# Two layers of a hybrid encoder on one core: x laid out by halves, the vectors loaded later, the first norm's sums on TensorE, factors spread by transposes

## The chip, the core and the metric

The kernel runs on one core of a Trainium2 chip. A core has TensorE (PE in the profile; PEld is its loading of stationary operands), VectorE (DVE), ScalarE (ACT), GpSimd (POOL) and SyncE (SP, which here only issues transfers). They run side by side and wait for each other through semaphores; each takes its instructions in order. Matmul results land in PSUM, which has eight banks of 128 x 512 f32 numbers; everything else lives in SBUF, with 128 partitions.

The metric is the time of one execution on the device in microseconds (us). Before the change it is 1564.54 us, the median of 3 runs (1564.0 to 1566.41).

## What is computed

```python
for l in range(DEPTH):                       # 2 layers, x is 512 tokens x 1024
    h = rms_norm(x, g_pre_mix[l])
    proj = h @ w_in[l]                       # 1024 -> 5632
    q_a, k_a, v_a, q_b, k_b, v_b, q_m, gate_pre = jnp.split(proj, splits, axis=-1)
    o_a = neighborhood_attention(..., rpb_na[l])      # 6 heads on an 8 x 64 grid
    o_b = dilated_attention(...)                      # 6 heads, three dilations
    o_m = memory_attention(..., mem_n, w_mem_kv[l])   # 4 heads over 256 memory tokens
    gates = jax.nn.sigmoid(gate_pre.reshape(B, S, N_BRANCH, D) + b_gate[l])
    merged = (gates[:, :, 0] * (o_a @ w_br_a[l]) + gates[:, :, 1] * (o_b @ w_br_b[l])
              + gates[:, :, 2] * (o_m @ w_br_m[l]))
    x = x + rms_norm(merged @ w_out[l], g_post_mix[l])
    h = rms_norm(x, g_pre_ffn[l])
    u = depthwise_conv_centred(h @ w_up[l], conv_w[l], conv_b[l])   # 1024 -> 2 x 2816, width 3
    a, b = jnp.split(u, 2, axis=-1)
    x = x + rms_norm((jax.nn.gelu(a) * b) @ w_down[l], g_post_ffn[l])
```

`mem_n` is the memory after a norm of its own. All numbers are float32.

## The kernel before

**Layout.** Everything is held transposed: features on the 128 partitions, the 512 tokens along the row. x is eight blocks (k = 0 to 7) of 128 features, in two tiles of 128 x 4 x 512. The tokens fall into two halves of 256 (`HALVES`).

**Products.** Each f32 operand is split into a high part in the type fp32r and the remainder (lo). A product is then three matmuls that add into one bank: hi by hi, hi by lo, lo by hi (`mm3`). A weight tile of 128 x 1024 (512 KB) is fetched by SP into `wraw` (three buffers), ACT casts its high part (`whi`), and DVE, or POOL where the call says `G`, subtracts to get the remainder (`wlo`). Tiles kept for later lie in the pools `m`, `h` and `ka`.

**Order.** The program's order on PE is written by a planner (`Woven`): the main loop emits projections, and jobs written as generators (norms, attention heads, the ends of sublayers) are spawned with a delay and run their next step when the planner's clock, advanced by a cost per matmul, has passed their due time. An instruction of a job therefore stands between the matmuls of the main loop. The other engines take their instructions in the order in which this one program emits them.

**Norms.** Squares are made on ACT, summed over k on DVE, and the sum over partitions is a product with `mean`, a column of 1/1024, so that tokens come to lie on the partitions (`rstd_job`). ACT takes the root, DVE the reciprocal. To bring the factor back onto a row of tokens for all partitions, the column is repeated 128 times as a stationary operand and multiplied with the identity in f32, 128 tokens at a time (lines 334 to 337); the profile shows two records for each such product. 18 such jobs run. `normed` then scales x by the gain (a column of `vec`) and the factor, and splits it.

**The start.** SP fetches the first half of x in four transfers, two weight tiles, the second half of x, and more weights. POOL's queue fetches the identity (`ident`) and the table `vec` of all gains, biases and convolution weights (128 x 464, 237 KB). `first_squares` makes eight squares of a half and sums them on DVE in two chains, so that PE gets two mean products of 256 tokens.

**The first projections of each layer.** Six of them (`FIRST`) run half by half in pairs (`run_group`), because the second half's norm is not done yet. `group_banks` gives the banks: the first pair in mm banks, the second in s banks, the third in the banks o and pt.

**Between the layers.** While layer 0's down projection runs, `mem_norm_job` prepares the memory norm of layer 1: eight squares on ACT, summed on POOL. The keys and values of the memory and the first projections of layer 1 follow. `end_job` closes a sublayer: it scales the result, adds it to x, and squares and sums the new x for the next norm.

**Values of the first attention.** `a_v` copies a projection from PSUM into a rearranged tile: one copy on ACT and two small ones on DVE, ahead of four transposes on PE. It runs six times.

Of the kernel before, what the change touches and what calls it, by code (L numbers as in the profile page):

```python
# [7 lines left out]
F32 = mybir.dt.float32  # L8
# [111 lines left out]
def tile_hybrid_encoder(ctx, tc, xT, memT, memg, vecs, rpb, w_in, w_kv, w_bra, w_brb, w_brm,  # L120
# [65 lines left out]

    xs = [const.tile([128, 4, 512], F32, name=f"x{i}") for i in range(2)]
    x = [xs[k // 4][:, k % 4, :] for k in range(KD)]

    def load_x(half):  # L190
        for k in range(0, KD, 2):
            nc.sync.dma_start(out=xs[k // 4][:, k % 4:k % 4 + 2, half], in_=xT[:, k:k + 2, half])

    load_x(HALVES[0])
    eps = const.tile([128, 1], F32, name="eps")
# [8 lines left out]
    vec = const.tile([128, depth, V_N], F32, name="vec")  # L204
    nc.gpsimd.dma_start(out=vec, in_=vecs)
    mg = const.tile([128, KD], F32, name="mg")
# [152 lines left out]
    def pre_norm_job(l, goff, acc, hs, i):  # L359
        half, box = HALVES[i], []  # L360
        yield from rstd_job(acc if isinstance(acc, list) else [acc[:, half]], 256, box)
        for k in range(KD):
            normed(x[k][:, half], vec[:, l, goff + k:goff + k + 1], box[0], hs[k][0][:, half], hs[k][1][:, half],
                   G if k in LOG[l > 0 and goff == V_PRE] else V)
# [8 lines left out]
    def end_job(l, goff, og, acc, acc2, i, then, lat, more=()):  # L373
# [3 lines left out]
        for k in range(KD):  # L377
            V.tensor_mul(og[k][:, half], og[k][:, half], box[0])
            (G if then is None and i and k in TAILG else V).tensor_add(x[k][:, half], x[k][:, half], og[k][:, half])
            if acc2 is not None:  # L380
                sumsq_add(acc2[:, half], x[k][:, half], k == 0, None, G if k in SQG[goff == V_POSTF] else V)
            else:
                nc.sync.dma_start(out=out[:, k, half], in_=x[k][:, half])
        if then is not None:
# [3 lines left out]
    def factor_end_job(l, goff, og, acc, acc2, i, nxt):  # L388
# [5 lines left out]
        for k in range(KD):  # L394
            V.tensor_mul(og[k][:, half], og[k][:, half], box[0])
            V.tensor_add(x[k][:, half], x[k][:, half], og[k][:, half])
            raw_split(l, gnext, k, x[k][:, half], h[k][0][:, half], h[k][1][:, half])
            if k == 0:
                yield 0.6
            wv.give(f"h{l}.{gnext}.{i}.{k}")  # L400
            yield 1.05
        for k in range(KD):
            sumsq_add(acc2[:, half], x[k][:, half], k == 0)
        yield 3.5
# [58 lines left out]
    def group_banks():  # L463
        return [mmbank(), mmbank(), sbank(), sbank(), obank(128), tbank()]

# [76 lines left out]
    def a_v(ps, qkv, flag):  # L542
# [282 lines left out]
    def first_squares(half):  # L825
        sqs = [ytile((128, 256)) for _ in range(KD)]
        for k in range(KD):
            ACT.activation(sqs[k], x[k][:, half], AF.Square)
# [21 lines left out]
    for l in range(depth):  # L850
# [8 lines left out]
        for pr in range(3):  # L859
            for i, evac in enumerate((a_q, a_k, a_v)):  # L860
                ps = pss[3 * pr + i] if pr < 2 else proj(l, 3 * i + pr, hs, fence if i < 2 else None)
                evac(ps, qkva, *([f"va{l}.{pr}"] if i == 2 else []))
# [143 lines left out]
def _layout(inputs):  # L1006
# [12 lines left out]
    a = {}  # L1019
    a["xT"] = np.ascontiguousarray(g["x"][0].T.reshape(KD, 128, SEQ).transpose(1, 0, 2))  # L1020
    a["memT"] = np.ascontiguousarray(g["mem"][0].T.reshape(KD, 128, N_MEM).transpose(1, 0, 2))
# [45 lines left out]
```

## Time and profile before

| | |
|---|---|
| median of 3 runs | 1564.54 us (1564.0 to 1566.41) |
| the profiled execution | 1565.1 us |
| its span in the profile | 1563.3 us, so 1.8 lie around it |
| mean granted clock of PE | 0.994 |
| ACT, DVE, POOL busy | 47%, 60%, 10% |
| moved by DMA | 144.90 MB, mean 93 GB/s |

All views below are of this one execution. Times count from the start of the span. A row of a timeline gives start and length of a run of equal instructions, the engine, the line of the program (L114 is the helper through which ACT and DVE are called, L242 the one for matmuls), the operation, destination and sources by their names in the program, the size, and the count. In brackets stands how long the engine had been idle just before, and what ended that. The granted clock is PE's, as a share of full speed.

### The profile page before, as it was taken

The page shows a single profiled execution, that of the slowest core. Times are in us where ns is not written, and L with a number is a line of the kernel's source. Part 1 is how long each engine was busy: PE and PEld are TensorE (multiplying, and loading weights), DVE is VectorE, ACT ScalarE, POOL GpSimd, SP SyncE. Part 2 cuts the span into 40 slices and gives each one's busy share as a digit, 9 for nine tenths or more (in the row PEclk, how much of TensorE's full clock was granted, in tenths as well). Part 3 has the DMA queues.
Part 4 walks back from the last instruction along what each step waited for, and adds up shares of the span by engine and source line. Part 5 has one row for each costly group of instructions (what it writes and reads, how often), then busy time and mean ns, then how long its engine had stood idle before and what let it go on. Part 6 is the DMA issues. An engine that isn't in the chain of part 4 may idle for free.

```text
span 1563.3 us, 20698 instructions
## 1 busy us (share of the span) xinstructions
PE 1524.4 (98%) x7994; PEld 1303.7 (83%) x7994; DVE 945.2 (60%) x1682; ACT 735.1 (47%) x1267; POOL 155.2 (10%) x219
## 2 busy tenths in 40 slices
PE   6999999999999999999989999999999999999997
PEld 6888888888988888788889888888889888888887
DVE  6685566235777777742385856753456877775233
ACT  5564575236544444522344645743364544444231
POOL 4340000210000000100061400001100000000000
PEclk9999999999999999999989999999999999999999
DMA  7222113325113322333331221132250222333331
GB/s 244 88 79 72 61 57 96 93 95 163 54 56 101 100 94 95 104 98 101 115 115 44 80 69 63 56 108 81 95 189 15 81 95 95 94 100 96 98 103 63
DMA packets 46610, 144.90 MB, mean 93 GB/s; under 512 B 5232, under 2 KB 11376, under 8 KB 46512
## 3 DMA queue, kind: packets, MB, share of 16 engines
q1 hardware_dynamic: 44656, 139.61, 28.2%
q10 hardware_dynamic: 1152, 2.10, 0.5%
q0 software_dynamic: 704, 1.88, 0.4%
q8 instruction: 62, 1.02, 0.3%
q14 instruction: 36, 0.29, 0.1%
HBM read 141.47 MB, written 2.10 MB: 92 GB/s over the span
## 4 chain that ended last, share of the span: by engine, by line
PE 54%; DVE 3%; issue 0%; ACT 0%; ACTq 0%; DVEq 0%
PE mm L242 48%; PE s L242 3%; PE o L242 2%; PE pt L242 1%; PE pt L253 1%; DVE y L114 1%; DVE x L114 1%; DVE m L114 0%; DVE acc L114 0%; DVE wlo L114 0%; DVE ka L114 0%; DVE st L114 0%; ACT sq L114 0%; ACT y L114 0%; ACT m L114 0%
## 5 line engine op out<-in xcount | busy, mean ns | idle before, releaser
L242 PE MATMUL mm<-h,whi 128*128 128x512 f32 x2496 | 775.7, 392 | 0.0
L242 PEld LDWEIGHTS mm<-h,whi 128*128 128x128 f32 x2496 | 461.5, 188 | 90.9
L242 PE MATMUL mm<-h,wlo 128*128 128x512 f32 x1248 | 486.4, 390 | 0.0
L114 DVE TENSOR_TENSOR wlo<-wraw,whi 128x1024 fp32r<-128x1024 f32 (+1 forms) x213 | 259.8, 1221 | 293.9 <-ACT whi L114 291.5
L114 ACT CAST whi<-wraw 128x1024 fp32r<-128x1024 f32 (+1 forms) x213 | 221.0, 1039 | 318.5 <-PE mm L242 310.4
L242 PEld LDWEIGHTS mm<-h,wlo 128*128 128x128 f32 x1248 | 234.3, 188 | 49.9
L242 PE MATMUL mm<-m,whi 128*128 128x512 f32 (+1 forms) x800 | 216.3, 358 | 2.7 <-ACT whi L114 1.8
L242 PEld LDWEIGHTS mm<-m,whi 128*128 128x128 f32 x800 | 142.5, 190 | 25.1 <-ACT whi L114 2.2
L242 PE MATMUL mm<-m,wlo 128*128 128x512 f32 (+1 forms) x400 | 142.8, 357 | 1.2 <-DVE wlo L114 1.2
L114 DVE SCALAR_TENSOR_TENSOR y<-y,vec,y 128x511 f32<-128x511 f32 x176 | 130.9, 750 | 3.5 <-ACT y L114 0.9
L114 DVE TENSOR_TENSOR y<-mm,R 128x512 f32<-128x512 f32 x82 | 56.4, 688 | 68.5 <-PE mm L242 68.5
L242 PEld LDWEIGHTS mm<-m,wlo 128*128 128x128 f32 x400 | 75.9, 190 | 12.5 <-DVE wlo L114 1.6
L766 POOL TENSOR_TENSOR m<-m,y 128x512 f32<-128x512 f32 x28 | 36.1, 1288 | 405.7 <-DVE y L114 405.7
L114 ACT ACTIVATE y<-y,vec 128x512 f32<-128x512 f32 x88 | 71.0, 813 | 2.2 <-DVE y L114 1.9
L242 PE MATMUL mm<-m,m 128*128 128x512 f32 x240 | 63.6, 395 | 0.0
L114 ACT ACTIVATE y<-y 128x512 f32<-128x512 f32 x44 | 27.8, 632 | 72.0 <-DVE y L114 71.5
L242 PE MATMUL s<-h,m 128*128 128x256 f32 x384 | 54.7, 290 | 5.4 <-DVE m L114 5.4
L114 ACT ACTIVATE y<-mm,vec 128x512 f32<-128x512 f32 (+1 forms) x91 | 57.4, 631 | 0.1
L242 PE MATMUL mm<-h,m 128*128 128x256 f32 x360 | 54.6, 298 | 2.8 <-DVE h L114 1.8
L114 ACT CAST m<-pt 128x512 fp32r<-128x512 f32 (+1 forms) x72 | 38.2, 539 | 40.4 <-PE pt L253 32.0
L114 DVE TENSOR_TENSOR acc<-acc,sq 128x256 f32<-128x256 f32 (+1 forms) x80 | 40.5, 507 | 26.2 <-ACT sq L114 24.6
L114 DVE TENSOR_TENSOR m<-pt,m 128x512 fp32r<-128x512 f32 (+1 forms) x72 | 45.0, 629 | 18.3 <-ACT m L114 17.4
(143 smaller groups left out, 1762.5 us busy)
## 6 DMA issues: line engine op xcount, KB each, us to landing
wraw<-in_w_in_dram SPq DMA_DIRECT2D x88, 512.0 KB, 3.4
wraw<-in_w_up_dram SPq DMA_DIRECT2D x88, 512.0 KB, 3.3
wraw<-in_w_down_dram SPq DMA_DIRECT2D x32, 512.0 KB, 3.5
wraw<-in_w_out_dram SPq DMA_DIRECT2D x16, 512.0 KB, 4.2
wraw<-in_w_down_dram SPq DMA_DIRECT2D x16, 384.0 KB, 3.1
wraw<-in_w_kv_dram SPq DMA_DIRECT2D x8, 512.0 KB, 4.4
wraw<-in_w_bra_dram SPq DMA_DIRECT2D x16, 192.0 KB, 2.3
x<-in_xT_dram SPq DMA_DIRECT2D x8, 256.0 KB, 6.9
```

What stands on the lines that cost most here:

```text
L114: return op(*args, **kw)
L242: wv.pe(nc.tensor.matmul(ps, a, b, start=first, stop=last), cost)
L253: wv.pe(nc.tensor.transpose(ps[:, 128 * i:128 * i + 128], s, ident), 0.11)
L766: (V if br == 2 and m >= 6 else G).tensor_add(acc[m], acc[m], gs)
```

## The change

1. x is one tile of 128 x 2 x 8 x 256, with the half as the outer index, in the chip's memory too, so that a transfer's run of numbers per partition is twice as long. The gains of the first norm come as a tile of their own, `g0` (128 x 8), first on ACT's queue. The whole table `vec` moves from POOL's queue to SP's, after the second half of x.
2. `first_squares` for the first half leaves four pair sums. PE makes four mean products, DVE two additions fewer.
3. Two products of a column of zeros, repeated, stand at PE's start, in the bank o (`idle(2)`).
4. The factor is spread by a transpose with the identity in place of a product, in all 18 jobs, with a planner's cost of 0.11 in place of 0.22.
5. The remainders of the first two weight tiles are both made on DVE; the second was on POOL.
6. `FIRST` and `group_banks` put the pair (4, 7), in the banks o and pt, ahead of the pair (6, 1), in the s banks.
7. The two small copies of `a_v` move from DVE to ACT.
8. The memory norm of layer 1 is spawned with a delay of 20 planner microseconds.

```diff
-FIRST = (0, 3, 6, 1, 4, 7)
+FIRST = (0, 3, 4, 7, 6, 1)
...
-    xs = [const.tile([128, 4, 512], F32, name=f"x{i}") for i in range(2)]
-    x = [xs[k // 4][:, k % 4, :] for k in range(KD)]
+    xs = const.tile([128, 2, KD, 256], F32, name="x")
+
+    def xh(k, half):
+        return xs[:, half.start // 256, k, :]
...
-            nc.sync.dma_start(out=xs[k // 4][:, k % 4:k % 4 + 2, half], in_=xT[:, k:k + 2, half])
+            i = half.start // 256
+            nc.sync.dma_start(out=xs[:, i, k:k + 2, :], in_=xT[:, i, k:k + 2, :])
+
+    g0 = const.tile([128, KD], F32, name="g0")
+    nc.scalar.dma_start(out=g0, in_=vecs[:, 0, V_PRE:V_PRE + KD])
     load_x(HALVES[0])
...
-    nc.gpsimd.dma_start(out=vec, in_=vecs)
...
-            mm(pr[:, 128 * b:128 * b + 128], spread, ident, True, True, 0.22)
+            wv.pe(nc.tensor.transpose(pr[:, 128 * b:128 * b + 128], spread, ident), 0.11)
...
+            g = g0[:, k:k + 1] if l == 0 and goff == V_PRE else vec[:, l, goff + k:goff + k + 1]
...
-        return [mmbank(), mmbank(), sbank(), sbank(), obank(128), tbank()]
+        return [mmbank(), mmbank(), obank(128), tbank(), sbank(), sbank()]
...
-        V.tensor_copy(vv[:, 0, :, 8:16], ps3[:, :, 0:8])
-        V.tensor_copy(vv[:, 0, :, 0:8], ps3[:, :, 56:64])
+        ACT.copy(vv[:, 0, :, 8:16], ps3[:, :, 0:8])
+        ACT.copy(vv[:, 0, :, 0:8], ps3[:, :, 56:64])
...
-            if k in (3, 5):
+            if k in (3, 5) and half != HALVES[0]:
                 V.tensor_add(sqs[k], sqs[k], sqs[k - 2])
-        return sqs[5::2]
+        return sqs[1::2] if half == HALVES[0] else sqs[5::2]
...
+    def idle(n):
+
+        one, none = mean[:, 0:1], zero[:, 0:1]
+        a, b = (bass.AP(t.tensor, t.offset, [list(t.ap[0]), [0, w]]) for t, w in ((one, 128), (none, 512)))
+        for _ in range(n):
+            mm(idle_bank, a, b, True, True, 0.0)
+
+    idle(2)
...
-    gw = group_weights([w_in[0, m] for m in FIRST[:2]], (V, G))
+    gw = group_weights([w_in[0, m] for m in FIRST[:2]], (V, V))
     load_x(HALVES[1])
+    nc.sync.dma_start(out=vec, in_=vecs)
...
-            wv.spawn(mem_norm_job(l + 1, hm, htile))
+            wv.spawn(mem_norm_job(l + 1, hm, htile), 20.0)
```

Three places in the engines' orders. A row names the line, the operation, destination and sources (the number behind a name counts the tiles) and the size of the destination.

**DVE at the start**, before: `y` are squares of the first half, `st` the factor, `m<-wraw,m` the remainder of a weight tile, `h_38` and `h_39` scaled blocks of x.

```order
L114 TENSOR_TENSOR y_125<-y_125,y_124 128x256
L114 TENSOR_TENSOR y_127<-y_127,y_126 128x256
L114 TENSOR_TENSOR y_127<-y_127,y_125 128x256
L114 TENSOR_TENSOR y_129<-y_129,y_128 128x256
L114 TENSOR_TENSOR y_129<-y_129,y_127 128x256
L114 TENSOR_TENSOR y_131<-y_131,y_130 128x256
L114 RECIPROCAL st_175<-st_175 128x2
L114 TENSOR_TENSOR m_149<-wraw_146,m_148 128x512
L114 SCALAR_TENSOR_TENSOR h_38_180<-x_85,vec,pt_170 128x256
```

The same place of the changed kernel:

```order
L114 TENSOR_TENSOR y_128<-y_128,y_127 128x256
L114 TENSOR_TENSOR y_130<-y_130,y_129 128x256
L114 TENSOR_TENSOR y_132<-y_132,y_131 128x256
L114 TENSOR_TENSOR y_134<-y_134,y_133 128x256
L114 RECIPROCAL st_181<-st_181 128x2
L114 SCALAR_TENSOR_TENSOR h_39_186<-x,g_86,pt_172 128x256
L114 TENSOR_TENSOR m_150<-wraw_147,m_149 128x512
L114 SCALAR_TENSOR_TENSOR h_40_190<-x,g_86,pt_172 128x256
L114 TENSOR_TENSOR m_154<-wraw_147,m_153 128x512
L114 TENSOR_TENSOR h_112<-h_39_186,h_111 128x256
L114 TENSOR_TENSOR m_160<-wraw_157,m_159 128x512
```

Two additions are gone, the first scaled block stands ahead of the first weight remainder, its gain comes from `g0` (printed as g_86), and a remainder of the second weight tile (wraw_157) has come to DVE.

**ACT at the start of layer 0's down projection**, before: `y` belongs to the last gelu block of the feed-forward, `h_1206` to `sq_1213` are the squares of the memory norm of layer 1, `whi` are casts of weights of the down projection.

```order
L114 ACTIVATE y_6051<-y_6049,vec 128x512
L114 ACTIVATE h_1206_6085<-h_6077 128x256
L114 ACTIVATE sq_1207_6087<-h_6077 128x256
L114 ACTIVATE sq_1208_6090<-h_6079 128x256
L114 ACTIVATE sq_1209_6093<-h_6079 128x256
L114 ACTIVATE sq_1210_6096<-h_6081 128x256
L114 ACTIVATE sq_1211_6099<-h_6081 128x256
L114 ACTIVATE sq_1212_6102<-h_6083 128x256
L114 ACTIVATE sq_1213_6105<-h_6083 128x256
L114 CAST ka_6057<-y_6045 128x512
L114 CAST whi_6131<-wraw_6129 128x1024
L114 CAST whi_6161<-wraw_6159 128x768
```

The same place of the changed kernel (the cast whi_6106 is that of whi_6131 before, whi_6136 that of whi_6161):

```order
L114 ACTIVATE y_6057<-y_6055,vec 128x512
L114 CAST whi_6106<-wraw_6104 128x1024
L114 ACTIVATE h_1220_6211<-h_6203 128x256
L114 ACTIVATE sq_1221_6213<-h_6203 128x256
L114 ACTIVATE sq_1222_6216<-h_6205 128x256
L114 ACTIVATE sq_1223_6219<-h_6205 128x256
L114 ACTIVATE sq_1224_6222<-h_6207 128x256
L114 ACTIVATE sq_1225_6225<-h_6207 128x256
L114 ACTIVATE sq_1226_6228<-h_6209 128x256
L114 ACTIVATE sq_1227_6231<-h_6209 128x256
L114 CAST ka_6063<-y_6051 128x512
L114 CAST whi_6136<-wraw_6134 128x768
```

One cast has moved from behind the eight squares to ahead of them; the next stays behind them.

**PE at the first projections of layer 1**, first half, before: the last product of the first pair (`mm`) and the start of the second (`s`).

```order
L242 MATMUL mm_7264<-h_7111,m_7018 128x256
L242 MATMUL s_7265<-h_7097,m_7225 128x256
L242 MATMUL s_7265<-h_7098,m_7225 128x256
L242 MATMUL s_7265<-h_7097,m_7226 128x256
L242 MATMUL s_7266<-h_7097,m_7235 128x256
L242 MATMUL s_7266<-h_7098,m_7235 128x256
```

The same place of the changed kernel:

```order
L246 MATMUL mm_7270<-h_7117,m_7027 128x256
L246 MATMUL o_7271<-h_7103,m_7231 128x256
L246 MATMUL o_7271<-h_7104,m_7231 128x256
L246 MATMUL o_7271<-h_7103,m_7232 128x256
L246 MATMUL pt_7272<-h_7103,m_7241 128x256
L246 MATMUL pt_7272<-h_7104,m_7241 128x256
```

The 48 products of the pair in o and pt now come ahead of the pair in s. 18 products of s follow them; then stands the mean product of the second half, 12 more of s, the spread, and the last 18.

More of the change, by code (lines that the diff above doesn't have):

```diff
@@ L362, in pre_norm_job @@
         for k in range(KD):
-            normed(x[k][:, half], vec[:, l, goff + k:goff + k + 1], box[0], hs[k][0][:, half], hs[k][1][:, half],
+            g = g0[:, k:k + 1] if l == 0 and goff == V_PRE else vec[:, l, goff + k:goff + k + 1]
+            normed(xh(k, half), g, box[0], hs[k][0][:, half], hs[k][1][:, half],
                    G if k in LOG[l > 0 and goff == V_PRE] else V)
@@ L378, in end_job @@
             V.tensor_mul(og[k][:, half], og[k][:, half], box[0])
-            (G if then is None and i and k in TAILG else V).tensor_add(x[k][:, half], x[k][:, half], og[k][:, half])
+            (G if then is None and i and k in TAILG else V).tensor_add(xh(k, half), xh(k, half), og[k][:, half])
             if acc2 is not None:
-                sumsq_add(acc2[:, half], x[k][:, half], k == 0, None, G if k in SQG[goff == V_POSTF] else V)
+                sumsq_add(acc2[:, half], xh(k, half), k == 0, None, G if k in SQG[goff == V_POSTF] else V)
             else:
-                nc.sync.dma_start(out=out[:, k, half], in_=x[k][:, half])
+                nc.sync.dma_start(out=out[:, k, half], in_=xh(k, half))
         if then is not None:
@@ L395, in factor_end_job @@
             V.tensor_mul(og[k][:, half], og[k][:, half], box[0])
-            V.tensor_add(x[k][:, half], x[k][:, half], og[k][:, half])
-            raw_split(l, gnext, k, x[k][:, half], h[k][0][:, half], h[k][1][:, half])
+            V.tensor_add(xh(k, half), xh(k, half), og[k][:, half])
+            raw_split(l, gnext, k, xh(k, half), h[k][0][:, half], h[k][1][:, half])
             if k == 0:
@@ L402, in factor_end_job @@
         for k in range(KD):
-            sumsq_add(acc2[:, half], x[k][:, half], k == 0)
+            sumsq_add(acc2[:, half], xh(k, half), k == 0)
         yield 3.5
@@ L1019, in _layout @@
     a = {}
-    a["xT"] = np.ascontiguousarray(g["x"][0].T.reshape(KD, 128, SEQ).transpose(1, 0, 2))
+    a["xT"] = np.ascontiguousarray(g["x"][0].T.reshape(KD, 128, 2, 256).transpose(1, 2, 0, 3))
     a["memT"] = np.ascontiguousarray(g["mem"][0].T.reshape(KD, 128, N_MEM).transpose(1, 0, 2))
```

5 lines of the change are left out of this document (3 added, 2 removed).

## The prediction

> **What bounds the kernel now.** I read the page's busy shares first, then the busy time of every engine by stretches of the span, and then the timelines of the stretches in which TensorE (PE) has gaps.
>
> ```profile
> span 1563.3 us, 20698 instructions
> PE 1524.4 (98%) x7994; PEld 1303.7 (83%) x7994; DVE 945.2 (60%) x1682; ACT 735.1 (47%) x1267; POOL 155.2 (10%) x219
> ```
>
> PE works 1524.4 of 1563.3 us, so a change that leaves PE's work alone can at most win the 38.9 us of gaps and what a low clock costs. The table by stretches (columns: stretch, its length, busy time with instructions for PE, PEld, DVE, ACT and POOL, granted clock, DMA share, GB/s) shows where both lie:
>
> ```profile
> 0.00:25.09 25.09, 12.56 (x67) 11.71 (x68) 15.11 (x34) 14.33 (x36) 9.64 (x37) 1.00 0.73 247
> 25.09:655.00 629.91, 625.00 (x3288) 533.56 (x3287) 414.05 (x740) 318.99 (x548) 60.74 (x70) 1.00 0.29 91
> 655.00:672.00 17.00, 13.98 (x54) 10.79 (x53) 7.96 (x7) 7.19 (x15) 6.98 (x7) 0.90 0.35 110
> 789.00:827.00 38.00, 31.20 (x235) 30.71 (x234) 28.53 (x68) 16.76 (x44) 19.85 (x38) 0.87 0.29 91
> 827.00:1553.00 726.00, 722.95 (x3748) 615.65 (x3747) 428.84 (x753) 336.09 (x559) 43.87 (x50) 1.00 0.27 86
> ```
>
> PE is idle 12.5 us in the head, 3.0 us at the start of layer 0's down projection (655 to 672), 6.8 us at the boundary of the layers (789 to 827), and 4.9 and 3.1 us spread over the two long stretches between. The remaining 8.6 us lie outside these rows and stay, as I see it, as they are. The two short ones also show a clock under 1. The change touches the head, both of these places, and a small product that recurs everywhere.
>
> The clock by windows of 3.41 us (the same columns) tells what a gap costs beyond itself:
>
> ```profile
> 666.12:669.53 3.41, 3.41 (x10) 2.66 (x9) 0.43 (x1) 0.00 (x0) 0.00 (x0) 0.50 0.86 226
> 789.00:792.41 3.41, 1.98 (x18) 1.81 (x17) 2.92 (x9) 2.53 (x8) 3.41 (x15) 1.00 0.49 156
> 792.41:795.83 3.42, 3.42 (x19) 3.42 (x18) 1.99 (x6) 1.02 (x4) 3.30 (x8) 0.50 0.17 24
> 809.48:816.31 6.83, 3.40 (x16) 3.43 (x17) 6.62 (x17) 3.20 (x8) 2.08 (x3) 0.50 0.50 166
> ```
>
> A window in which PE was busy 1.98 of 3.41 us is followed by one at half clock. At half clock a product of 256 columns takes 3.40/16 = 0.213 us. At full clock it is 0.120 (48 in the 5.92 us of the row at 826.51 below, less a last one of some 0.28). One window at 0.50 therefore loses 3.41 x (1 - 0.120/0.213) = **1.49 us**.
>
> **The head.** The timeline (start, duration, engine, operation, and in brackets the idle time ahead with its releaser):
>
> ```profile
> 0.75 1.97 SPq L192 DMA_DIRECT2D x<-in_xT_dram  x4
> 2.01 0.54 POOL L205 DMA_DIRECT2D vec<-in_vecs_dram  x1
> 3.51 1.42 ACT L114 ACTIVATE y<-x 128x256 f32<-128x256 f32 x4 [1.26 <-DMA x<-in_xT_dram]
> 8.31 0.72 ACT L114 ACTIVATE y<-x 128x256 f32<-128x256 f32 x2 [0.33 <-DMA x<-in_xT_dram]
> 12.69 0.48 DVE L114 SCALAR_TENSOR_TENSOR h<-x,vec,pt 128x256 f32<-128x256 f32 x1 [0.29 <-PE pt L242]
> 13.09 1.53 DVE L114 TENSOR_TENSOR m<-wraw,m 128x512 fp32r<-128x512 f32 x1
> 16.08 7.33 PE L242 MATMUL mm<-h,m 128*128 128x256 f32 x41 [1.84 <-DVE h L114]
> 20.40 2.56 ACT L114 ACTIVATE y<-x 128x256 f32<-128x256 f32 x8
> 23.50 1.05 PE L242 MATMUL pt<-mean,y 128*128 128x1 f32 x8
> ```
>
> The first half of x comes in four transfers. The squares of the first two run from 3.51 without a break, 0.71 us per transfer; those of the last wait until 8.31. In between the table vec (128 x 464 numbers, 237 KB) had been issued at 2.01. With vec behind x, and each transfer in pieces of 2 KB, I let the last two transfers follow at 0.8 us each: squares of the last at 5.8 instead of 8.31. The bounds: at 0.71 each it is 5.6; if something other than vec held them, 8.31 stays.
>
> From there to the first scaled tile were 12.69 - 8.31 = 4.38 us. Four records of the mean product move off this path, because the first three pairs are summed before the last lands, and two of the four spread records go. I take 0.4 us for each pair of records (2 x 0.213): 12.69 becomes 5.8 + 4.38 - 0.8 = 9.4, a gain of 3.3. DVE then also subtracts the second weight tile, which POOL did: two more subtractions. The row at 13.09 prices one at 1.53 beside POOL's; the 128x256 operation at 12.69 takes 0.48, so 128x512 alone cannot be far under it. Most of it lies beside products at half clock, which need 6 x 0.213 = 1.28 us per k of this pair. I charge 0.3, up to 2 x 1.53. The gain of 3.0 to 3.3 carries over to the squares of the second half (20.40) and its mean product (23.50), which stand in order behind it. Against it stands one half-clock window that I expect with even odds, 0.75. **Head: -2.5**, from -0.5 (x no earlier) to -4.2 (no subtraction felt, clock kept). The two zero products at the start lie ahead of 3.5 us, where PE has nothing: 0.
>
> **The start of the down projection.** Eight squares of layer 1's memory norm stand in ACT's order ahead of the cast of the next weights.
>
> ```profile
> 655.84 0.61 PE L242 MATMUL mm<-m,whi 128*128 128x512 f32 x2
> 657.80 1.67 ACT L114 ACTIVATE sq<-h 128x256 f32<-128x256 f32 x5
> 661.06 0.39 PE L242 MATMUL mm<-m,wlo 128*128 128x512 f32 x1
> 662.17 1.77 ACT L114 CAST whi<-wraw 128x1024 fp32r<-128x1024 f32 x2
> 663.26 0.74 PE L242 MATMUL mm<-m,whi 128*128 128x512 f32 x2 [1.81 <-ACT whi L114]
> 663.38 3.17 DVE L114 TENSOR_TENSOR wlo<-wraw,whi 128x1024 fp32r<-128x1024 f32 x2
> 671.92 0.62 PE L242 MATMUL mm<-ka,whi 128*128 128x512 f32 x2
> ```
>
> One piece of 24 products ran from 655.84 to 661.29 (0.227 each). The next 24 ran from 661.29 to 671.92, 10.63 us: their weights were cast only from 662.17, because the squares, paced by POOL's sums, ran before it; and a half-clock window followed (666.12 above). With the cast ahead of the squares it starts at about 657.6 and takes 1.77/2 = 0.89, and the subtraction, 3.17/2 = 1.6, ends at about 660.2, before the product at 661.3 that needs the first of it. Then the 24 take 24 x 0.227 = 5.4. **-5.2**; the bounds are 0 (squares late elsewhere, below) and -5.2, since the piece cannot go faster. Spawned 20 us later, the squares meet casts that PE needs less soon; the following piece's cast stands behind them in the new order and would have 664.2 as its start, against 666.7 when PE reaches it.
>
> **The boundary.** In layer 1's first projections the pair in the s banks moves to the end.
>
> ```profile
> 791.52 0.58 PE L242 MATMUL pt<-mean,acc 128*128 128x1 f32 x4 [1.43 <-DVE acc L114]
> 807.01 0.52 PE L242 MATMUL s<-h,m 128*128 128x256 f32 x3
> 812.35 0.41 DVE L114 TENSOR_TENSOR m<-s,m 128x256 fp32r<-128x256 f32 x1
> 812.91 7.13 PE L242 MATMUL s<-h,m 128*128 128x256 f32 x45 [5.37 <-DVE m L114]
> 815.97 1.30 DVE L114 TENSOR_TENSOR acc<-acc,sq 128x256 f32<-128x256 f32 x2 [0.20 <-ACT sq L114]
> 821.32 0.50 PE L242 MATMUL pt<-mean,acc 128*128 128x1 f32 x4
> 826.51 5.92 PE L242 MATMUL mm<-h,m 128*128 128x256 f32 x48
> ```
>
> After three products into the first s bank PE waits 5.37 us, at half clock through to 816.31. What ends the wait is no weight but the second s bank: DVE reads it at 812.35 to split the memory's values (`m<-s,m`), and until then it is taken. The pair in o and pt needs no s bank, and its weights now stand where those of the s pair stood, of which the first was used at 807.01. So it fills the hole: 48 x 0.120 = 5.8 us, to 812.8, when the s bank is free. Then, in the new order, 18 products of s run to 814.9, and the mean product of the second half has to wait: the chain of sums on DVE ends at 815.97 + 1.30 = 817.3, some 0.5 later with the copies' share, 817.8. So **the wait removed is replaced by one of 2.9 us**. Behind it stand 0.45 for the mean product, 12 products, the spread (0.22) and 18 more: 30 x 0.120 = 3.6. That ends at 822.1, against 826.51: 4.4 won. A gap of 2.9 leaves PE at most 0.5 us in one window, or splits over two; I charge one half-clock window, 1.49. **-2.9**, from 0 (the banks o and pt, or the weights of their pair, late as well) to -4.4.
>
> The Trainium skill, page "TensorE: Matmul & The Clock Gate", section "HAM oscillation — how this bites in real kernels", only warns of idle gaps above about 3.4 us. By it a wait of 2.9 costs no clock, and the sum would be 1.49 lower. This trace disagrees: the gap of 1.43 us ahead of 791.52 was followed by a window at 0.50.
>
> **The spreads and the copies.** Spread products against transposes in the table of groups and the timeline, and the copies of the attention values:
>
> ```profile
> L242 PE MATMUL pt<-ident,st 128*128 128x128 f32 x72 | 12.4, 298 | 1.8 <-DVE st L114 1.8
> L253 PE MATMUL pt<-ident,sq 128*128 128x128 f32 x48 | 7.2, 273 | 2.4 <-DVE sq L114 2.4
> 77.39 0.60 PE L253 MATMUL pt<-ident,sq 128*128 128x128 f32 x4
> 78.76 0.35 DVE L114 COPY sq<-pt 128x64 f32<-128x64 f32 x2
> 79.26 0.63 PE L253 MATMUL pt<-ident,sq 128*128 128x128 f32 x4 [1.28 <-DVE sq L114]
> ```
>
> 72 records are 18 jobs of four: two products, each of two records. Four transposes leave four records, one each, and start (0.60 - 0.273)/3 = 0.109 apart (273 ns is the mean of one). Two records fewer per job are 0.22 us; 16 jobs stand outside the head: **-3.5**, from -2 (some stand beside a wait) to -4.
>
> At 79.26 PE waits 1.28 us for copies on DVE that start only after its other work; on ACT they follow the large copy at once. There are 12 copies in 6 jobs; PE's gap is of this kind in two or three of them: **-0.6**, from +0.5 (ACT's queue is later) to -0.8. Shifts of the order elsewhere: 0, from -1.5 to +1.5.
>
> **Sum.** -2.5 - 5.2 - 2.9 - 3.5 - 0.6 = -14.7. The profiled run took 1565.1, 0.6 above the median of 1564.54 and 1.8 above its span; 1564.54 - 14.7 = **1549.8**.
>
> **Rivals.**
> A. The weights at 662 come no earlier, because the squares only move into other casts: the term of -5.2 shrinks to 0 and the rest stays, 1555.0. For it: the squares must run somewhere, 8 of them at the pace of POOL. Against it: the new order puts the cast first. Chance 0.14.
> B. The new waits cost no clock, neither in the head (0.75) nor at the boundary (1.49): 1547.5. The window after 789.00 speaks against it. For it: a wait of 2.9 that is split evenly over two windows leaves each about as busy as the one at 789.00, no emptier. Chance 0.16. The rule of the Trainium skill that is named above would give this time at the boundary.
> C. Slower: x is now one tile instead of two. If the sums of x on DVE then wait for ACT's squares of the same tile, each of eight sums waits some 0.42 us, 3.4 per job, and in five jobs PE stands behind: +17 - 14.7 gives 1567. It decides as soon as every sum waits for a square. Against it: the new order shows no such wait, and four blocks shared each tile before, with squares and sums of different blocks in it. Chance 0.04.
> D. Little is gained: x arrives no earlier, and both waits come back in other places; only the spreads are left, 1561 to 1564. Chance 0.06, half of it within 0.2%.
>
> **How the numbers follow.** My forecast has the remaining 0.60. A measurement of this kernel can tell about 0.2%, 3.1 us. Only D's upper half (0.03) and parts of C and mixed cases lie within it: same 0.05, slower 0.04, faster 0.91. The range has B and A inside, with the bounds of the head, the boundary and the order around them: 1545.0 to 1557.0; outside remain C, D and the sum of all best ends, some 0.15.
>
> **What would show it.** In the new profile the first scaled tile should stand at about 9.4 and the last squares of x's first half at 5.8. The piece after 661 should take 5.4 to 6 us without a gap for whi. At the boundary the hole of 5.37 should be gone, with a wait of about 3 us ahead of the mean product and one window at 0.50. The group of the spreads should have 36 records, not 72. I am wrong if vec did not hold x, if the squares delay a later cast, or if the pair in o and pt has to wait as well.

## The result and the profile after

The changed kernel took **1552.8 us**, the median of 4 runs (1551.81 to 1555.18), against 1564.89 before (4 runs): a ratio of 0.9924, 95% interval 0.9907 to 0.9941, or 12.1 us less. The forecast was 1549.8, with a range of 1545.0 to 1557.0. Five more runs of the same kernel in a later session had a median of 1551.83 (1550.08 to 1554.6).

The profiled execution after is the slowest of its four (1555.18 us). The first lines of its page:

```profile
span 1553.4 us, 20653 instructions
## 1 busy us (share of the span) xinstructions
PE 1525.1 (98%) x7970; PEld 1302.2 (84%) x7970; DVE 940.6 (61%) x1670; ACT 735.9 (47%) x1279; POOL 150.7 (10%) x216
```

The span is 9.9 us shorter, while PE's busy time has not fallen (1524.4 before), although 36 records of spreads are gone: 3.8 us of it are the products of zeros at the start, which lie where PE had waited before. Without them its work is 3.1 us less, and the other 6.8 of the 9.9 us are time of gaps. To see where, I took the start of each matmul in both traces and subtracted. The table gives what was won in each stretch; its places are times of the profile before. The second column is the profiled execution of the result, the third one of the very same kernel in a later run (`again` below, span 1548.5).

| stretch (us, before) | forecast | result | again |
|---|---|---|---|
| to 56.5: head and layer 0's first projections | 2.5 | 0.2 | 2.6 |
| 56.5 to 661 | spreads, copies | 1.1 | 1.1 |
| 661 to 671.9: the piece of 24 products | 5.2 | 5.2 | 5.2 |
| 671.9 to 802.5 | spreads | 0.5 | 1.0 |
| 802.5 to 843.8: boundary | 2.9 | 1.7 | 3.8 |
| 843.8 to the last spread | spreads, copies | 1.4 | 1.3 |
| sum | 14.7 | 10.1 | 15.0 |

Up to 790 us the middle of the kernel gives the same in both executions. The head and the boundary don't.

**The head** in the timeline of the result:

```profile
6.38 0.72 ACT L114 ACTIVATE y<-x 128x256 f32<-128x256 f32 x2 [1.36 <-DMA x<-in_xT_dram]
8.76 0.72 ACT L114 ACTIVATE y<-x 128x256 f32<-128x256 f32 x2 [1.65 <-DMA x<-in_xT_dram]
12.28 0.48 DVE L114 SCALAR_TENSOR_TENSOR h<-x,g,pt 128x256 f32<-128x256 f32 x1 [0.78 <-PE pt L341]
20.27 2.56 ACT L114 ACTIVATE y<-x 128x256 f32<-128x256 f32 x8
23.37 1.05 PE L246 MATMUL pt<-mean,y 128*128 128x1 f32 x8 [1.47 <-DVE y L114]
```

x's last transfer is squared at 8.76, not at 5.8: it comes even later than before (8.31). From there to the first scaled block it takes 12.28 - 8.76 = 3.52 us instead of 4.38, so the shorter path is there with its 0.86.

**The down projection's start**, ACT and PE:

```profile
656.14 1.03 ACT L114 CAST whi<-wraw 128x1024 fp32r<-128x1024 f32 x1
657.39 1.33 ACT L114 ACTIVATE sq<-h 128x256 f32<-128x256 f32 x4
659.93 0.62 PE L246 MATMUL mm<-m,whi 128*128 128x512 f32 x2
665.37 0.62 PE L246 MATMUL mm<-ka,whi 128*128 128x512 f32 x2
```

The cast stands ahead of the squares. The piece begins at 659.93 and the next one at 665.37: 5.44 us, without a gap, where there were 10.63.

**The boundary**, PE:

```profile
805.47 0.52 PE L246 MATMUL pt<-h,m 128*128 128x256 f32 x3
805.83 2.32 PE L246 MATMUL s<-h,m 128*128 128x256 f32 x18
810.45 0.89 PE L246 MATMUL pt<-mean,acc 128*128 128x1 f32 x4 [2.30 <-DVE acc L114]
814.19 3.80 PE L246 MATMUL s<-h,m 128*128 128x256 f32 x18
```

The pair in o and pt runs up to 805.83 and the s bank is free by then. The wait for the chain of sums is there, 2.30 us. The 18 products at 814.19 take 3.80 us, so they run at half clock.

**Spreads and copies**, by group and by one place of each:

```profile
L341 PE MATMUL pt<-ident,st 128*128 128x128 f32 x36 | 8.1, 310 | 1.5 <-DVE st L114 1.5
L257 PE MATMUL pt<-ident,sq 128*128 128x128 f32 x48 | 7.3, 274 | 1.7 <-ACT sq L114 1.7
418.02 0.38 PE L341 MATMUL pt<-ident,st 128*128 128x128 f32 x2
418.16 0.61 PE L246 MATMUL s<-h,m 128*128 128x256 f32 x3
```

The same place before:

```profile
418.70 0.60 PE L242 MATMUL pt<-ident,st 128*128 128x128 f32 x4
419.06 0.96 PE L242 MATMUL s<-h,m 128*128 128x256 f32 x6
```

36 records instead of 72. From the first record of a spread to the next product it takes 0.14 us, where the same place took 0.36 before. PE's wait for the copies fell from 2.4 to 1.7 us.

**The clock** is the main difference between the two executions. Windows of the result around its wait of 1.47, ahead of 786.65 and around the wait of 2.30 (stretch, length, busy time with instructions of PE, PEld, DVE, ACT and POOL, granted clock, DMA share, GB/s):

```profile
22.06:25.48 3.42, 2.11 (x18) 2.11 (x19) 2.29 (x7) 2.82 (x8) 1.54 (x2) 1.00 0.24 74
25.48:28.90 3.42, 3.42 (x19) 3.42 (x18) 2.19 (x5) 1.88 (x5) 1.16 (x1) 0.50 0.72 236
783.24:786.65 3.41, 1.76 (x13) 1.59 (x13) 2.62 (x8) 2.19 (x7) 3.41 (x12) 1.00 0.49 156
807.14:810.55 3.41, 1.11 (x10) 0.94 (x9) 2.95 (x8) 1.17 (x3) 1.27 (x2) 1.00 0.31 119
810.55:813.96 3.41, 3.41 (x17) 3.41 (x18) 0.17 (x1) 0.26 (x1) 1.53 (x3) 0.50 0.13 38
813.96:817.37 3.41, 3.41 (x18) 3.41 (x17) 2.80 (x7) 1.19 (x3) 2.10 (x3) 0.50 0.00 0
```

And the boundary of `again`, where the same wait (2.41 us) fell across the edge of a window:

```profile
803.29:806.70 3.41, 2.03 (x17) 1.83 (x16) 3.34 (x10) 1.48 (x4) 0.11 (x1) 1.00 0.61 192
806.70:810.12 3.42, 2.39 (x20) 2.42 (x21) 0.93 (x3) 0.37 (x2) 2.65 (x4) 1.00 0.06 12
```

In the result the wait lies in one window, PE is busy 1.11 us in it, and two windows at half clock follow. In `again` each of two windows keeps 2.03 and 2.39, and none follows.

### The profile page after: what moved, and what is told of

It is laid out like the page before. It is cut to its first block, busy times and chain, and to the rows that moved or that the text cites. A ratio compares the mean times of both kernels' runs of the same rounds, so it can differ in the third digit from the quotient of the medians.

```text
span 1553.4 us, 20653 instructions
## 1 busy us (share of the span) xinstructions
PE 1525.1 (98%) x7970; PEld 1302.2 (84%) x7970; DVE 940.6 (61%) x1670; ACT 735.9 (47%) x1279; POOL 150.7 (10%) x216
## 4 chain that ended last, share of the span: by engine, by line
PE 92%; DVE 5%; ACT 1%; issue 1%; DMA 0%; SPq 0%; ACTq 0%; DVEq 0%
PE mm L246 80%; PE s L246 5%; PE o L246 4%; PE pt L257 2%; PE pt L246 1%; DVE y L114 1%; DVE m L114 1%; DVE x L114 1%; ACT y L114 0%; DVE acc L114 0%; DVE ka L114 0%; DMA x<-in_xT_dram 0%; DVE wlo L114 0%; ACT m L114 0%; PE pt L341 0%
## 5 line engine op out<-in xcount | busy, mean ns | idle before, releaser
L114 DVE TENSOR_TENSOR acc<-acc,sq 128x256 f32<-128x256 f32 (+1 forms) x80 | 41.3, 517 | 27.2 <-ACT sq L114 25.7
```

The source lines that it names most:

```text
L114: return op(*args, **kw)
```

## The experiments

Each kernel ran in 5 rounds beside the kernel before (o_delay has 6 runs, best 4). All differences are to the changed kernel's 1552.8 unless another is named. Over all nine runs of the changed kernel the median is 1552.21; by that base a loss is 0.6 larger and a gain 0.6 smaller.

**u_delay: the memory norm without its delay**

```diff
-            wv.spawn(mem_norm_job(l + 1, hm, htile), 20.0)
+            wv.spawn(mem_norm_job(l + 1, hm, htile))
```

> The changed kernel with the memory norm of layer 1 spawned without its delay of 20, so that the eight squares stand ahead of the cast again. Theory (the gain at 661 comes from this cast alone): the piece of 24 products after about 660 takes 10 to 11 us again, with gaps released by whi and a window at 0.50; the time is 5 to 6.5 us above the changed kernel's 1552.8, so 1558 to 1559.5. Rival (the squares cost as much at the later place, so the gain is smaller than the local one): 1554 to 1556.

1556.99 (1555.47 to 1559.09; ratio to before 0.9949, 0.9935 to 0.9963), **+4.2**. ACT and PE at the place:

```profile
661.13 1.78 ACT L114 CAST whi<-wraw 128x1024 fp32r<-128x1024 f32 x2
662.22 0.73 PE L246 MATMUL mm<-m,whi 128*128 128x512 f32 x2 [1.82 <-ACT whi L114]
664.15 0.79 PE L246 MATMUL mm<-m,wlo 128*128 128x512 f32 x1 [1.19 <-DVE wlo L114]
```

The cast is at 661 again and both waits are back. The time lies between the two theories. The profiled execution shows where the rest went: it is 5.3 us behind the result's one at the end of this piece, still 5.2 at 785, and 1.8 from 834 to the end. So all that came back came back at the boundary, where it had no half-clock window and the result's had three from 786 on. Whether that follows from the edit, or from where the windows fell, is not shown.

**o_delay: the same delay alone, in the kernel before**

```diff
-            wv.spawn(mem_norm_job(l + 1, hm, htile))
+            wv.spawn(mem_norm_job(l + 1, hm, htile), 20.0)
```

> The kernel before with the delay of 20 for the memory norm alone. Theory (the prediction's second term): the piece behind 661 runs in 5.4 to 6 us, and 5 to 6 of these stay to the end, 1559 to 1560. Rival (undoing it in the changed kernel cost 4.2 us at the end where 6.0 were lost on the spot, since later waits take back some): 1561 to 1562.5.

1558.84 (1557.8 to 1559.12; 0.9963, 0.995 to 0.9976) against 1564.96 beside it: **-6.1**, a little more than the theory's 5 to 6. The piece of 24 products runs from 660.64 to 666.08, 5.44 us as in the result. One argument of one call is half of the whole change.

**u_banks: the order of the pairs as before**

```diff
-FIRST = (0, 3, 4, 7, 6, 1)
+FIRST = (0, 3, 6, 1, 4, 7)
...
-        return [mmbank(), mmbank(), obank(128), tbank(), sbank(), sbank()]
+        return [mmbank(), mmbank(), sbank(), sbank(), obank(128), tbank()]
```

> The changed kernel with FIRST and the banks in the order of before. Theory (the s bank, read late by the memory's values, is what PE waited for, and the pair in o and pt fills the hole): a wait of about 5 us released by DVE m comes back after three s products, and the wait ahead of the second half's mean product of 2.3 us goes; the boundary costs 2.7 us more, so 1555.5. Rival (both waits cost the clock alike, and the sum of norm and bank is the same chain on DVE): within 1 us of 1552.8.

1554.91 (1553.18 to 1557.18; 0.9937, 0.9925 to 0.995), **+2.1**. PE:

```profile
804.54 7.82 PE L246 MATMUL s<-h,m 128*128 128x256 f32 x45 [5.27 <-DVE m L114]
814.36 0.51 PE L246 MATMUL pt<-mean,acc 128*128 128x1 f32 x4
```

The wait for the s bank is back with 5.27 us and that of the mean product is gone, as the theory says. The size is within what executions differ by, so the 2.7 is not confirmed to a microsecond. The profiled execution has four half-clock windows between 20 us and the tail, as the result's has, and a span 0.9 longer (1554.3), although x's last transfer was squared 1.4 us earlier (7.37); so the order of the pairs costs some 2.3 there, if the earlier x carries through.

**u_spread: f32 products in place of the transposes**

```diff
-            wv.pe(nc.tensor.transpose(pr[:, 128 * b:128 * b + 128], spread, ident), 0.11)
+            mm(pr[:, 128 * b:128 * b + 128], spread, ident, True, True, 0.11)
```

> The changed kernel with f32 products in place of the transposes, at the same planner cost, so that PE's order is the same. Theory (each job costs 0.23 us more on PE, which is the bound): the rows of pt<-ident,st are 72 again, the place of one takes 0.36 us instead of 0.135, and the time is 3.5 to 4 us up, 1556.5. Rival (most of it disappears in waits elsewhere): 1553 to 1554.5.

1558.71 (1556.05 to 1560.78; 0.9958, 0.9945 to 0.9971), **+5.9**, more than either theory. PE's order is the same, but ACT's and DVE's is not: the scheduler, which orders these two by modelled times, changed them at many places, in the head and in later norms. One of them is the second cast of the third weight tile, now ahead of the second half's squares; u_idle, below, shows what that can cost. So this run prices the transposes only together with these changes. On the spot, a spread took 0.36 us again (421.45 to 421.81).

**u_vec: the table vec back at the start**

```diff
+    nc.gpsimd.dma_start(out=vec, in_=vecs)
...
-    nc.sync.dma_start(out=vec, in_=vecs)
```

> The changed kernel with the table vec on POOL's queue at the start again. The prediction's step (vec held x back): the squares of the last two transfers of x's first half start 1 to 2 us later than the changed kernel's 6.38 and 8.76. Rival, as the changed kernel's profile suggests (something else holds them, vec is not felt): 6 to 7.3 and 8 to 9 as before and after, and the time within 1 us of 1552.8.

1552.63 (1550.59 to 1554.81; 0.9921, 0.9908 to 0.9933), **the same**. The squares of x's last transfer:

```profile
8.27 0.72 ACT L114 ACTIVATE y<-x 128x256 f32<-128x256 f32 x2 [1.89 <-DMA x<-in_xT_dram]
```

With vec in front the last squares are no later than without it (8.76), and those of the transfer before it start at 5.66, not later than 6.38 either. The prediction's step on vec falls.

**x_alone: POOL's two other transfers out of the way**

```diff
-    nc.gpsimd.dma_start(out=ident, in_=c_ident)
+    nc.sync.dma_start(out=ident, in_=c_ident)
...
-    nc.gpsimd.dma_start(out=mg, in_=memg)
...
     nc.sync.dma_start(out=vec, in_=vecs)
+    nc.sync.dma_start(out=mg, in_=memg)
```

> The changed kernel with POOL's two transfers at the start moved to SP's queue: ident between the first half of x and the weights, mg behind vec. So the first half of x shares the start with g0 alone. Theory (one of the sixteen shares of x's last transfer hangs behind transfers of other queues): the squares of the last transfer start at 5.6 to 6.3 instead of 7.4 to 9.1, and the head ends 2 us earlier, 1550.5 to 1551.5. Rival (the share is late for a reason that has nothing to do with these queues): 7.4 to 9.1 as in the other runs, time within 1 us of 1552.8.

1553.58 (1552.03 to 1554.86; 0.993, 0.9916 to 0.9944): no gain in the median. In its profile x was earlier, though:

```profile
6.52 0.72 ACT L114 ACTIVATE y<-x 128x256 f32<-128x256 f32 x2 [0.36 <-DMA x<-in_xT_dram]
21.24 0.94 PE L245 MATMUL pt<-mean,y 128*128 128x1 f32 x7 [1.93 <-DVE y L114]
```

The mean product of the second half came 2.1 us before that of the result. Four half-clock windows stood behind it, one of them at 22.6. That is as many as in the result, and the span, 1551.4, is 2.0 below the result's: in this execution the earlier x was kept to the end. When x landed in the other four runs is not on record. ACT's and DVE's orders differ at some places in the head, too.

**u_idle: without the products of zeros**

```diff
-    idle(2)
```

> The changed kernel without the two products of zeros at the start. Theory (they lie where PE has nothing to do, and what clock they win is gone before the first products on h): the first window at full clock (5.0 to 8.4) goes, the time stays within 1 us of 1552.8. Rival (they are worth a window further on): 1554 to 1556.

1555.96 (1555.47 to 1556.78; 0.9946, 0.9932 to 0.9959), **+3.2**: against the theory and against my forecast of nothing. PE at the second half's mean product, and the clock there:

```profile
22.71 0.61 PE L246 MATMUL pt<-mean,y 128*128 128x1 f32 x4 [2.00 <-DVE y L114]
24.11 1.01 PE L246 MATMUL pt<-mean,y 128*128 128x1 f32 x4 [0.80 <-DVE y L114]
...
20.10:23.51 3.41, 1.21 (x9) 0.92 (x8) 3.34 (x8) 2.78 (x8) 1.06 (x1) 1.00 0.69 264
23.51:26.92 3.41, 2.81 (x13) 2.81 (x14) 1.67 (x4) 1.75 (x5) 1.68 (x2) 0.50 0.29 67
26.92:30.34 3.42, 3.42 (x18) 3.42 (x18) 2.28 (x6) 1.76 (x5) 3.08 (x3) 0.50 0.77 264
```

PE waits twice for DVE's sums, 2.8 us together, and two half-clock windows follow. Both orders changed at this place: ACT casts, and DVE subtracts, one more half weight tile ahead of the squares and sums. Whether the order or the clock was the cause took another run.

**u_idle_pin: the same, with the order held**

```diff
-            split(raw[:, k:k + c, :], hi, lo, eng)
+            split(raw[:, k:k + c, :], hi, lo, eng)
+            behind(last_copy[0], after if k else None)
...
-            ACT.activation(sqs[k], xh(k, half), AF.Square)
+            last_sq[0] = ACT.activation(sqs[k], xh(k, half), AF.Square).ins
...
-    idle(2)
...
-    gw += group_weights([w_in[0, m] for m in FIRST[2:]], (V, G, V, G))
+    gw += [weights(w_in[0, FIRST[2]], KD, 128, big, V, last_sq[0])] + group_weights([w_in[0, m] for m in FIRST[3:]], (G, V, G))
```

> The changed kernel without the products of zeros, and with the second cast of the third weight tile held behind the second half's squares on ACT, where it stands in the changed kernel (without the products of zeros alone, it had moved ahead of them). Theory 1 (the 3.2 us lost without these products come from that order): within 1 us of 1552.8, and the mean product of the second half starts by 23.4. Theory 2 (they come from the clock that the products win): 1555 to 1556.5 again.

1551.05 (1549.94 to 1552.36; 0.9914, 0.9899 to 0.9929), **4.9 below u_idle** and 0.8 below the changed kernel run beside it (1551.83). So the order was the cause, and the products of zeros at the start are worth nothing that these runs can tell. (The order is held but for one cast and one subtraction, which changed places with a neighbour.) The profiled executions differ by four half-clock windows, two of them at the boundary, so only the medians price the order. PE at the second half's mean product:

```profile
23.37 1.05 PE L247 MATMUL pt<-mean,y 128*128 128x1 f32 x8 [0.94 <-DVE y L114]
```

**again: the changed kernel once more**

> The changed kernel once more, unchanged, beside the next two. Theory (the half-clock windows behind the waits start where they fall, so that executions differ by whole windows of 1.49 us): runs between 1550.5 and 1555.5 again, the median within 1 us of 1552.8, and x's last transfer landing between 7.3 and 9.1. Rival (the difference between executions lies elsewhere): two executions with the same windows at 0.50 differ by more than 1.5 us.

1551.83 (1550.08 to 1554.6; 0.9918, 0.9902 to 0.9933). x's last transfer was squared at 7.92. Its profiled execution has one half-clock window between 20 us and the tail, at 782.8, the result's has four (one after 25, one after 786, two after 810). The spans are 1548.5 and 1553.4: 4.9 us apart. By the table 2.4 of it lie in the head, where one window is missing (1.49) and x was 0.84 earlier, and 2.1 at the boundary, where two are missing. These two give less than 2 x 1.49; at full clock PE comes to wait for DVE's scaled blocks there (0.29 us ahead of the product at 815.03).

u_vec's execution has three windows and a span of 1551.0; the three executions with the one near 784 alone (`again`, u_idle_pin and fill2) have 1548.5 to 1549.3. The rival stays untested for the changed kernel itself: its two traced executions have different windows.

**fill: products of zeros at three waits**

```diff
         half, box = HALVES[i], []
+        if l > 0 or i > 0:
+            idle(1 + l * i, obank(128) if i == 0 else mmbank())
         yield from rstd_job(acc if isinstance(acc, list) else [acc[:, half]], 256, box)
...
-    def idle(n):
+    def idle(n, bank=None):
...
-            mm(idle_bank, a, b, True, True, 0.0)
+            mm(idle_bank if bank is None else bank, a, b, True, True, 0.0)
```

> The changed kernel with the zero products also at three waits: one ahead of the mean product of the second half at the start (PE waited 1.47 us there), one ahead of that of layer 1's first half (1.55), two ahead of that of layer 1's second half (2.30). They write a bank that nobody reads. Theory (a wait costs its own length and, through the half-clock windows behind it, about as much again): the windows at 0.50 after 25, 786 and 810 us, four in the changed kernel's profile, go away and the waits stay; 4 x 1.49 = 6.0 at most, likely 3 to 5, so 1548 to 1550. Rival (waits this short cost no clock, and products of zeros don't count as work for it): no window goes, 1552.8 or up to 1 us above.

1550.89 (1550.3 to 1552.58; 0.9916, 0.9902 to 0.993), **-1.9**. In its profiled execution no half-clock window was left between 18.6 us and the tail. That fits products of zeros that count as work for the clock, but doesn't show it alone, since `again` has one window without them. The gain is smaller than the theory's and within what executions differ by, and one of the three places had changed ACT's and DVE's order at the boundary.

**best: both of these**

This is fill with x_alone's two moved transfers.

> The changed kernel with both: the products of zeros at three waits, and POOL's two transfers on SP's queue. Theory (x's last transfer lands 1 to 2 us earlier, and without half-clock windows behind the later waits this is kept to the end): 1.5 us below the 1550.9 of the products of zeros alone, so 1549 to 1549.8. Rival (moving the two transfers wins nothing, as in its run alone at 1553.6): 1550.5 to 1552.

1550.95 (1549.84 to 1552.52; 0.9912, 0.9897 to 0.9928): the rival. And x's last transfer was late again. A half-clock window came back at 786.10, behind a window with 1.99 us busy: PE waited 1.40 us for the factor there (at 785.86), and no product of zeros stands in that wait. ACT at the start and PE's clock:

```profile
7.80 0.72 ACT L114 ACTIVATE y<-x 128x256 f32<-128x256 f32 x2 [1.39 <-DMA x<-in_xT_dram]
...
786.10:789.51 3.41, 3.41 (x18) 3.41 (x17) 3.12 (x8) 1.19 (x3) 2.99 (x8) 0.50 0.52 157
```

**fill2: products of zeros at two waits, with unchanged orders**

```diff
+        if i > 0:
+            idle(1 + l, mmbank())
```

`idle` takes the bank as in fill.

> The changed kernel with the products of zeros at two of the three waits, at the start's second half (one) and at layer 1's second half (two). Without the one in between, the orders of ACT and DVE are those of the changed kernel, row for row. Theory (only the half-clock windows behind the two waits are taken away, and nothing else moves): no window at 0.50 near 25 and 810, that near 786 stays; executions lie closer together and below 1552, the median at 1549.5 to 1550.5. Rival (the products of zeros cost what they save): 1551.5 to 1552.5.

1550.88 (1549.56 to 1551.36; 0.9913, 0.99 to 0.9927). PE and the clock at the boundary:

```profile
805.93 1.88 PE L246 MATMUL mm<-zero,mean 128*128 128x512 f32 x4
808.52 0.58 PE L246 MATMUL pt<-mean,acc 128*128 128x1 f32 x4 [0.71 <-DVE acc L114]
...
804.60:808.00 3.40, 3.21 (x17) 1.90 (x15) 3.19 (x10) 1.47 (x4) 0.62 (x1) 1.00 0.40 155
808.00:811.40 3.40, 2.88 (x24) 2.91 (x25) 1.05 (x4) 0.26 (x1) 2.15 (x4) 1.00 0.16 42
```

The same wait stands there, 1.9 us of it filled, and the clock stays up; without the filling the first of the two windows would hold 3.21 - 1.88 = 1.33 us of work. Only the window near 784 is left. The runs lie within 1.8 us of each other, where the changed kernel's nine spread over 5.1 (1550.08 to 1555.18, median 1552.21). By the medians this is 1.3 us better. But the kernel before was faster beside it, too (1563.28): fill2 is 12.4 below that, where the changed kernel was 12.1 (the result) and 13.9 (`again`) below the one beside it. The intervals of the ratios overlap, so it is the fastest version found (with fill and best beside it), but not one shown to be faster.

## Why the prediction held, and where it failed

The direction, the range and the largest term were right, and the forecast was 3.0 us too low. That the sum of `again`, 15.0, is so near to the forecast's 14.7 is in part luck: it has a larger gain at the boundary and another reason for the head's.

- **The down projection's start, -5.2.** Right to the tenth on the spot (5.2 in both executions). Alone it gives -6.1, and undoing it costs +4.2. Rival A, that the squares only move into other casts, is out.
- **The head, -2.5.** The step that failed is "With vec behind x, and each transfer in pieces of 2 KB, I let the last two transfers follow at 0.8 us each: squares of the last at 5.8 instead of 8.31". The trace has the time at which each of a transfer's sixteen parts lands. In the result the first parts of the four transfers do come at this pace, at 2.98, 3.74, 4.65 and 5.53 us. vec was felt here, too: the last transfer's first part landed at 6.2 to 6.6 us with vec in front (the kernel before, o_delay, u_vec) and at 5.3 to 5.7 in the eleven executions without. But the squares wait for the last of the sixteen parts, and without vec that came between 7.3 and 9.0 us (6.5 in x_alone), with it between 8.2 and 8.6. That is the wait that the prediction left out, and it is no later in the executions with vec in front.

  The shorter path behind x's last transfer was worth 0.86 (0.8 forecast). From the first scaled block to the squares of the second half it is 7.99 us (20.27 - 12.28) instead of 7.71, 0.28 for the added subtractions and what else moved there (0.3 forecast). That leaves about 0.6 to the second half's mean product when x lands at the same time. `again` still shows 2.6 by the end of the first projections. Beside this 0.6 and an x that landed 0.4 earlier, shorter spreads are in it, and a gain that I had not seen. The memory norm's spread had waited for its factor in the kernel before, and in `again` and the result it does not. As many products, twelve, stand between the mean product and the spread in all three; but before, DVE took the reciprocal only behind two subtractions. PE and DVE at this place before:

```profile
45.15 0.71 PE L242 MATMUL pt<-ident,st 128*128 128x128 f32 x4 [0.68 <-DVE st L114]
42.12 2.90 DVE L114 TENSOR_TENSOR wlo<-wraw,whi 128x1024 fp32r<-128x1024 f32 x2
44.94 0.15 DVE L114 RECIPROCAL st<-st 128x2 f32<-128x2 f32 x1
```

  The same place in `again`, where the subtractions are over earlier:

```profile
42.90 0.38 PE L341 MATMUL pt<-ident,st 128*128 128x128 f32 x2
39.90 2.35 DVE L114 TENSOR_TENSOR wlo<-wraw,whi 128x1024 fp32r<-128x1024 f32 x2
42.17 0.15 DVE L114 RECIPROCAL st<-st 128x2 f32<-128x2 f32 x1
```

- **The boundary, -2.9.** The mechanism is right in each of its steps: s bank, filled hole, a new wait for the sums. The wait was 2.30 to 2.41, forecast 2.9. What was mis-sized is the clock behind it: I charged one window, the result had two (1.7 won) and `again` none (3.8 won, less than the 4.4 forecast without a window: PE then waits for DVE behind it).
- **Spreads, -3.5, and copies, -0.6.** 0.36 to 0.14 us per spread, times 16, is 3.5, and the waits for copies fell by 0.7. The stretches that hold little else won 1.1, 0.5 and 1.4 (1.0 and 1.3 in `again`), 3.0 to 3.4 together; twelve of the 18 spreads lie in them, and 12 x 0.22 + 0.7 is 3.3.
- **The products of zeros, 0.** Right by themselves, but only with the orders held: taking them out moved a cast on ACT and a subtraction on DVE, and that cost 4.9 us between u_idle and u_idle_pin.
- **Rival B, no clock lost at the new waits.** It is what `again` shows at the boundary and the result does not. The rule weighed there, of the Trainium skill's page "TensorE: Matmul & The Clock Gate", section "HAM oscillation — how this bites in real kernels", warns only of gaps above about 3.4 us. It fails here more often than I allowed for: 1.47 us of waiting were enough at 25 us, 1.54 at 782 in `again`.
- **Rivals C and D** did not come true; DVE's waits of sums for squares are 25.7 us in all, where they were 24.6 before, and no lasting return of the old waits was seen.

What stays open is the last part of x's last transfer. In the result ten of its sixteen parts had landed by 6.4 us, five more came between 6.8 and 7.8, and the last at 8.7. With ident and mg out of the way all had landed by 6.5 in one execution (x_alone); in the other (best) fourteen had by 6.3, and two came at 7.7 and 7.8. What holds these parts is not shown.

## What to carry to other kernels

- On an engine that takes its work in order, look for what stands ahead of a cast or split that the bound engine needs next. Here eight squares that nobody waited for cost five to six microseconds, and a delay on one call removed them.
- Where the bound engine waits one or two microseconds, count the clock behind the wait too, and in windows: the same kernel's executions differ by whole windows, according to where the wait falls. A difference of two kernels is only read after their windows are counted.
- If a scheduler decides the order of the other engines, compare the orders of every experiment before its time is given to the edit.

## What was not expected of the hardware

- A half-clock window can follow a window in which PE was busy 2.11 of 3.42 us, and may not follow one with 2.03 of 3.41. Other runs are further apart: in u_banks one followed 2.47 us, in u_idle_pin none followed 1.54. The share of busy time as the profile gives it has no clean limit here. The two places, u_banks first:

```profile
21.05:24.46 3.41, 2.47 (x21) 2.48 (x22) 1.95 (x6) 2.81 (x8) 1.90 (x2) 1.00 0.27 82
24.46:27.87 3.41, 3.41 (x19) 3.41 (x17) 2.83 (x7) 2.15 (x5) 1.12 (x2) 0.50 0.73 246
804.69:808.10 3.41, 1.54 (x13) 1.34 (x12) 3.20 (x10) 1.52 (x4) 0.70 (x2) 1.00 0.46 178
808.10:811.51 3.41, 2.96 (x25) 2.99 (x26) 1.05 (x4) 0.33 (x2) 2.07 (x4) 1.00 0.12 38
```

- After a window with 1.11 us busy there were two windows at half clock, the second behind one in which PE was busy throughout (810.55 to 813.96). That is no rule: in u_vec only one followed a window with 1.08 us busy (806.50 to 809.93), and after the 1.76 us of the window ahead of 786.65 there was one, too.
- Products of zeros seem to count as work for the clock: with 1.88 us of them in a wait, no window followed (fill2). At the start, where PE did little else, two of them were followed by full clock for the window from 5.0 to 8.4 us in the result, and so it is in eight of the ten traced executions that begin with them; in x_alone and fill2 the profile records full clock only from 15.8 and 19.6 us.
